# Moving the scaling of fifteen output columns from VectorE to GpSimd, with new splits of the last two row blocks

One core of one Trainium2 chip. The metric is the device time of one execution in microseconds (us); lower is better.

## The reference

```python
x: float32 [32, 512, 1024]; divisor = 1024.0
out = (np.sum(x, axis=-1) / divisor).astype(np.float32)      # [32, 512]
```

That is 16,384 sums of 1,024 floats. 67.11 MB are read and 0.07 MB written, so the kernel should cost what the input stream costs, plus a short tail behind the last bytes.

## The kernel before

Each of the 128 partitions holds 128 rows: 112 in the main part, then sixteen "last" ones. VectorE sums most rows with a reduce, ScalarE the others with an activation that accumulates. The loads get smaller towards the end: eight rows, four, two, then `row` (one row for each partition, shared between the two engines), then the last row in three pieces `pa`, `pb`, `pc`. All loads are on SyncE's queue. Cuts are marked `# ...`.

```python
    bulk = ctx.enter_context(tc.tile_pool(name="bulk", bufs=3))      # 14 rows each
    one = ctx.enter_context(tc.tile_pool(name="one", bufs=1))
    # ...
    res = one.tile([P, M], F32, name="res")          # M = 112 main rows
    fin = one.tile([P, L], F32, name="fin")          # L = 16 last rows
    q = one.tile([P, L], F32, name="q")
    r = one.tile([P, L], F32, name="r")
    nc.gpsimd.memset(r, 0.0)
    # ... main part; then loads and sums of 8, 4 and 2 rows into q (tiles t, t4, t2) ...
    c = 768
    row = one.tile([P, D], F32, name="row")
    load(row, x_last[:, j, :])
    act_sum(r[:, j : j + 1], row[:, c:], by=scale)                                   # ScalarE
    nc.vector.reduce_sum(out=q[:, j : j + 1], in_=row[:, :c], axis=AX)

    a, b = 448, 704
    pa = one.tile([P, a], F32, name="pa")
    pb = one.tile([P, b - a], F32, name="pb")
    pc = one.tile([P, D - b + 2], F32, name="pc")
    load(pa, x_last[:, L - 1, :a])
    load(pb, x_last[:, L - 1, a:b])
    load(pc[:, : D - b], x_last[:, L - 1, b:])
    # ... res scaled on GpSimd and stored ...
    act_sum(pc[:, D - b : D - b + 1], pa)                                            # ScalarE
    nc.vector.reduce_sum(out=pc[:, D - b + 1 :], in_=pb, axis=AX)
    nc.vector.scalar_tensor_tensor(
        out=fin[:, : L - 1], in0=q[:, : L - 1], scalar=scale, in1=r[:, : L - 1], op0=MULT, op1=ADD
    )
    scaled = one.tile([P, D - b + 2], F32, name="scaled")
    nc.vector.tensor_scalar(                                                         # "L198"
        out=scaled, in0=pc, scalar1=scale, scalar2=0.0, op0=MULT, op1=ADD, accum_out=fin[:, L - 1 :]
    )
    tc.keep_in_program_order(nc.sync.dma_start(out=o_last, in_=fin))
```

The sums of `pa` and `pb` are written behind the bytes of `pc`, so L198 scales and adds up everything of the last row. It therefore needs three things: pa's sum (ScalarE), pb's sum (VectorE) and pc's landing (DMA).

Two helpers run when the program is finished. `latest_wait_first` sorts the semaphore waits of an instruction; those that do not fit on it are asked for by an instruction ahead of it on the same sequencer. `close_while_storing` puts the checks of all other engines ahead of the last store.

```python
    def rank(i, w):
        own = {"DVE": "DVE_", "Activation": "Activation_", "SP": "DVE_", "Pool": "DVE_"}
        if w.ant_name.startswith("DMAHW") and i.engine != SP:
            return 0
        return 1 if w.ant_name.startswith(own.get(...)) else 2      # cut
```

## Time and profile before

| What | Before |
|---|---|
| median of 3 runs | 161.5 us (161.36 to 161.5) |
| span of the profiled run | 159.8 us |
| last landing of `row` | 156.16 us |
| last store issued | 158.31 us, 2.155 us after row's landing |

The span of the profiled execution, as the profile counts it, is 1.55 us shorter than its device time of 161.31 us. The time up to row's landing is the stream. The 2.155 us behind it are the tail, which is all that computation can still shorten. The page, the chain and the timeline of this kernel stand in the prediction below.

### The profile page before, as it was taken

What the parts mean: (1) busy time and instruction counts of PE and PEld (TensorE: products, weight loads), DVE (VectorE), ACT (ScalarE), POOL (GpSimd) and SP (SyncE); (2) the same over time, 40 slices, a digit from 0 to 9 for tenths busy, and PEclk for the clock granted to TensorE, in tenths of its full rate; (3) what the DMA queues carried; (4) which work ended last, traced back from release to release, by engine and by line L of the source; (5) the groups of instructions that cost most, each with busy time, mean ns of one, the idle gap of its engine ahead of it and who ended that gap; (6) DMA issues with size and microseconds to landing.
All of it is one profiled execution on the core that took longest, in us unless ns stands there. A gap on an engine that the chain in (4) does not pass through costs nothing.

```text
span 159.8 us, 139 instructions
## 1 busy us (share of the span) xinstructions
DVE 121.1 (76%) x17; ACT 19.6 (12%) x37; POOL 0.8 (0%) x6
## 2 busy tenths in 40 slices
DVE  0500059995999599978999599959995996494985
ACT  3000000000000000000000000000001900480973
POOL 0000000000000000000000000000000000001000
DMA  7999999978999999978999999978999999899993
GB/s 250 472 459 459 459 459 459 459 330 359 459 459 459 459 459 459 459 316 373 459 459 459 459 459 459 416 345 388 459 459 427 394 480 505 353 435 390 408 400 132
DMA packets 2592, 67.18 MB, mean 420 GB/s; under 512 B 544, under 2 KB 928, under 8 KB 1056
## 3 DMA queue, kind: packets, MB, share of 16 engines
q1 hardware_dynamic: 2592, 67.18, 98.0%
HBM read 67.11 MB, written 0.07 MB: 420 GB/s over the span
## 4 chain that ended last, share of the span: by engine, by line
DMA 76%; DVE 22%; SPq 1%; issue 0%; DVEq 0%
DMA t<-in_x_dram 56%; DMA row<-in_x_dram 21%; DVE res L153 20%; SPq L142 1%; DVE q L176 1%; DVE scaled L198 0%; DVE pc L193 0%; DVE fin L194 0%; DVEq L198 0%; DVEq L232 0%
## 5 line engine op out<-in xcount | busy, mean ns | idle before, releaser
L153 DVE TENSOR_REDUCE res<-t 128x14 f32<-128x14336 f32 (+3 forms) x9 | 111.2, 12360 | 34.3 <-DMA t<-in_x_dram 34.3
L147 ACT ACTIVATE junk<-t 128x1024 f32<-128x1024 f32 x16 | 16.2, 1013 | 135.9 <-DMA t<-in_x_dram 135.9
L153 DVE TENSOR_REDUCE q<-t 128x4 f32<-128x4096 f32 (+2 forms) x3 | 7.9, 2642 | 2.7 <-DMA t<-in_x_dram 2.5
L147 ACT ACTIVATION_READ_ACCUMULATOR junk<-t 128x1 f32 x16 | 3.0, 187 | 0.0
L147 ACT ACT_TABLE_LOAD x1 | 1.3, 1283 | 1.7 <-PEq L218 1.7
L189 POOL TENSOR_SCALAR res<-res 128x112 f32<-128x112 f32 x1 | 0.5, 494 | 143.8 <-DVE res L153 143.8
L176 DVE TENSOR_REDUCE q<-row 128x1 f32<-128x768 f32 x1 | 1.0, 953 | 0.0
L198 DVE TENSOR_SCALAR_CACHE_REDUCE scaled<-pc 128x322 f32<-128x322 f32 x1 | 0.5, 490 | 0.1
L147 ACT ACTIVATE junk<-pa 128x448 f32<-128x448 f32 x1 | 0.5, 548 | 0.0
L193 DVE TENSOR_REDUCE pc<-pb 128x1 f32<-128x256 f32 x1 | 0.4, 414 | 0.0
L147 ACT ACTIVATE junk<-row 128x256 f32<-128x256 f32 x1 | 0.4, 388 | 0.1
L194 DVE SCALAR_TENSOR_TENSOR fin<-q,r 128x15 f32<-128x15 f32 x1 | 0.2, 176 | 0.0
L147 ACT ACTIVATION_READ_ACCUMULATOR junk<-pa 128x1 f32 x1 | 0.2, 186 | 0.0
L147 ACT ACTIVATION_READ_ACCUMULATOR junk<-row 128x1 f32 x1 | 0.2, 185 | 0.0
L139 POOL MEMSET r<- 128x16 f32 x1 | 0.1, 112 | 1.3 <-POOLq L218 1.3
L218 POOL MEMSET const-bfloat16-1.0<- 128x1 bf16 x1 | 0.1, 103 | 0.0
L218 POOL MEMSET const-uint8-127<- 128x1 uint8 x1 | 0.1, 102 | 0.0
L218 POOL MEMSET const-float32-0.0<- 128x1 f32 x1 | 0.1, 99 | 0.2 <-issue 0.2
L218 POOL MEMSET const-float32-1.0<- 128x1 f32 x1 | 0.1, 99 | 0.0
L198 DVE DVE_READ_ACCUMULATOR scaled<-pc 128x1 f32 x1 | 0.1, 83 | 0.0
## 6 DMA issues: line engine op xcount, KB each, us to landing
t<-in_x_dram SPq DMA_DIRECT2D x7, 7168.0 KB, 35.7
t<-in_x_dram SPq DMA_DIRECT2D x1, 6144.0 KB, 33.3
t<-in_x_dram SPq DMA_DIRECT2D x1, 4096.0 KB, 26.1
t<-in_x_dram SPq DMA_DIRECT2D x2, 1024.0 KB, 18.6
t<-in_x_dram SPq DMA_DIRECT2D x1, 2048.0 KB, 30.5
row<-in_x_dram SPq DMA_DIRECT2D x1, 512.0 KB, 33.2
pa<-in_x_dram SPq DMA_DIRECT2D x1, 224.0 KB, 33.3
pc<-in_x_dram SPq DMA_DIRECT2D x1, 160.0 KB, 33.1
```

What stands on the lines that cost most here:

```text
L139: nc.gpsimd.memset(r, 0.0)
L142: tc.keep_in_program_order(nc.sync.dma_start(out=dst, in_=src))
L147: nc.scalar.activation(junk[:, :n], src, COPY, scale=by, accum_out=dst)
L153: nc.vector.reduce_sum(out=dst[:, :d], in_=t[:, :d, :], axis=AX)
L176: nc.vector.reduce_sum(out=q[:, j : j + 1], in_=row[:, :c], axis=AX)
L189: nc.gpsimd.tensor_scalar_mul(out=res, in0=res, scalar1=scale)
L193: nc.vector.reduce_sum(out=pc[:, D - b + 1 :], in_=pb, axis=AX)
L194: nc.vector.scalar_tensor_tensor(out=fin[:, : L - 1], in0=q[:, : L - 1], scalar=scale, in1=r[:, : L - 1], op0=MULT, op1=ADD)
L198: nc.vector.tensor_scalar(out=scaled, in0=pc, scalar1=scale, scalar2=0.0, op0=MULT, op1=ADD, accum_out=fin[:, L - 1 :])
L218: nc = _bacc.Bacc("TRN2", target_bir_lowering=False, num_devices=1)
```

## The change

Its intent: take the scaling of the fifteen columns out of VectorE's chain at the end, and re-split the last blocks so that VectorE gets less and ScalarE more. The memset of `r` is not needed any more, so `r` becomes one column.

```diff
-    r = one.tile([P, L], F32, name="r")
-    nc.gpsimd.memset(r, 0.0)
+    r = one.tile([P, 1], F32, name="r")
-    c = 768
+    c = 688
-    act_sum(r[:, j : j + 1], row[:, c:], by=scale)
+    act_sum(r, row[:, c:], by=scale)
-    a, b = 448, 704
+    a, b = 480, 672
-    nc.vector.scalar_tensor_tensor(
-        out=fin[:, : L - 1], in0=q[:, : L - 1], scalar=scale, in1=r[:, : L - 1], op0=MULT, op1=ADD
+    nc.gpsimd.tensor_scalar_mul(out=fin[:, :j], in0=q[:, :j], scalar1=scale)
+    nc.gpsimd.tensor_scalar(
+        out=fin[:, j : j + 1], in0=q[:, j : j + 1], scalar1=scale, scalar2=r, op0=MULT, op1=ADD
     )
```

## The prediction

> **What bounds the kernel now.** I read the page from the top, then the waits, then the end of the timeline and the landing records. The kernel sums 16,384 rows of 1,024 floats: 67.11 MB come in, 0.07 MB go out. The first thing to see is that the change cannot touch most of the span.
>
> ```profile
> span 159.8 us, 139 instructions
> DVE 121.1 (76%) x17; ACT 19.6 (12%) x37; POOL 0.8 (0%) x6
> q1 hardware_dynamic: 2592, 67.18, 98.0%
> HBM read 67.11 MB, written 0.07 MB: 420 GB/s over the span
> ```
>
> The DMA queue is busy for 98.0% of the span. VectorE (DVE) has 76%, ScalarE (ACT) 12%, GpSimd (POOL) under 1%. So the stream of input sets about 156 us, and what can be tuned is the tail behind the last loads. The chain that ended last, in order of time, shows how long that tail is (columns: start us, us, what):
>
> ```profile
> 122.91 33.25 DMA row<-in_x_dram
> 156.16 0.02 issue
> 156.18 0.96 DVE q L176
> 157.14 0.03 issue
> 157.17 0.18 DVE fin L194
> 157.34 0.34 DVE pc L193
> 157.68 0.04 DVEq L198
> 157.72 0.07 issue
> 157.79 0.49 DVE scaled L198
> 158.28 0.01 DVEq L232
> ```
>
> Here is the reader's main finding: from 156.18 to 158.28 VectorE runs without a real gap: the row ahead (L176), the scaling of fifteen columns (L194), the middle piece (L193), and the scaling with sum of the last piece (L198). Then SyncE issues the store at 158.31, which lands at 159.73; the span ends at 159.76. The landing records (the last of a load's sixteen increments) are: row 156.16, pa 156.70, pb 157.02, pc 157.50. So pb lay ready 0.24 us before VectorE began on it, and pc lay ready 0.29 us before L198 began. VectorE's own chain is late, not the data. ScalarE is not late either (timeline, ACT):
>
> ```profile
> 156.18 0.39 ACT L147 ACTIVATE junk<-row 128x256 f32<-128x256 f32 x1
> 156.50 0.18 ACT L147 ACTIVATION_READ_ACCUMULATOR junk<-row 128x1 f32 x1
> 156.72 0.55 ACT L147 ACTIVATE junk<-pa 128x448 f32<-128x448 f32 x1
> 157.20 0.19 ACT L147 ACTIVATION_READ_ACCUMULATOR junk<-pa 128x1 f32 x1
> ```
>
> Its last result is signalled at 157.40, also 0.39 us before L198. So the change has something to gain, but no more than the distance from 157.79 down to the next limit: pc at 157.50 plus the start of an instruction.
>
> **What the Trainium skill says.** (1) "VectorE: DVE Perf Modes", section "The perf-mode tier table": a reduce runs at one element a cycle. The trace agrees: 1,024 columns take 1,220 ns and 768 take 953 ns, a slope of 1.04 ns a column, with about 150 ns fixed. (2) "SBUF — State Buffer", section "Who interferes with whom": a VectorE instruction with two SBUF inputs contends with a GpSimd one that reads SBUF, while a reduce and the tensor_scalar form that writes out its accumulator do not. The tail of before has no GpSimd work, so no run yet shows it; but the 490 ns of L198 for 322 columns (322 x 1.04 = 335, plus 155) fits one element a cycle. The new GpSimd instructions should therefore delay nothing on VectorE, and the one two-input instruction there disappears. (3) "ScalarE: Activation LUTs", section "What ACT_TABLE_LOAD costs": an ACTIVATE with immediate scale and bias costs 186 ns + 0.833 ns a column. The trace has 388 ns for 256 and 548 ns for 448: exactly 0.833 ns a column, with 175 ns fixed; I use the trace. (4) "Perfetto Trace Analysis", section "GPSIMD Engine Instruction": a GpSimd instruction's reported span is unreliable. The trace cannot test that, so I leave its duration a wide margin below.
>
> **The change part by part.** I rebuild the tail from the landing of row at 156.16. The bytes ahead of it are the same, so I keep this time.
>
> Landings. pa grows by 32 columns (16 KB), pb shrinks by 64, pc grows by 32; the sum is the same. pb's 128 KB took 157.02 - 156.70 = 0.32 us, so 16 KB is 0.04 us. Hence pa lands at 156.74, pb at 156.98, and pc at 157.50 as before.
>
> VectorE. The row ahead has 688 columns instead of 768: 80 x 1.04 = 83 ns less, 870 instead of 953 ns, so it ends at 157.05. The scaling (L194) is gone: it held the chain for 0.18 us, and with it goes its 0.03 us start. In before, L193 could start 0.09 us before the end of the instruction ahead of it (157.26 against 157.34), as it had no wait on that one; now 157.05 - 0.09 = 156.96 comes before pb's landing, so pb's landing at 156.98 plus 0.02 for the start decides: 157.00. It reduces 192 columns: 414 - 64 x 1.04 = 347 ns, end 157.35, signalled 157.36.
>
> ScalarE. The row's part grows to 336 columns: 388 + 80 x 0.833 = 455 ns, and its accumulator is read by 156.76. pa landed at 156.74, so its ACTIVATE starts about 156.76, some 0.04 us later than before. It takes 548 + 32 x 0.833 = 575 ns, and by the spacing of before (start to signal 0.677 us, plus 0.027) the sum is signalled at about 157.465, 0.07 us later than before.
>
> The last instruction needs three things: pb's sum (157.36), pc's bytes (157.50) and pa's sum (157.465). In before it started 0.105 us after the signal of its last compute input (157.683 to 157.788). After: 157.465 + 0.105 = 157.57; for pc's landing 157.50 + 0.02 = 157.52. So L198 starts at 157.57, not 157.79: 0.22 us earlier. It handles 354 columns instead of 322: 32 x 1.04 = 33 ns more, 523 ns. It signals 0.54 us after its start, at 158.11, against 158.295. **Sum: 0.22 - 0.03 = 0.185 us gained**, and the fixed end (issue, store, closing) behind it is unchanged.
>
> The same by terms: removing L194 and the smaller row and pb would free about 0.32 us of VectorE time (157.465 against 157.79). ScalarE's larger shares take back 0.10 of it, as the pa sum becomes the last input, and the larger pc takes 0.03.
>
> GpSimd. The first new instruction (fourteen columns) needs nothing later than 156.15, the end of the reduce before the row. The second (one column, r as a per-partition scalar) needs the row's sum at 157.06. GpSimd started 0.08 us after such a signal in before (145.57 to 145.65), so at 157.14. The only size I have is this group:
>
> ```profile
> L189 POOL TENSOR_SCALAR res<-res 128x112 f32<-128x112 f32 x1 | 0.5, 494 | 143.8 <-DVE res L153 143.8
> ```
>
> As an upper estimate I take the full 494 ns for one column: done at about 157.65. The store needs it at 158.11, so 0.45 us of slack stay; even twice the estimate would cost only a few hundredths. The kernel's closing code makes SyncE check the other engines and the stored main result (landed 157.71) before the last store, which in before was passed at about 157.77. This is also under 158.11.
>
> At the other end the memset of r goes (112 ns at 1.7 us), beside a first load that lands at 4.8 us: worth nothing.
>
> **The rivals.** (A) GpSimd takes the place of L194 as the end of the chain. For: [...]a scalar read from memory, and a producer finishing at 157.06 only. Against: 0.45 us of slack and a 112-column instruction of the same kind at 494 ns. If the small one took 1.2 us, the store would leave at about 158.4 and the time would be 161.6, no gain. (B) The split was better before: ScalarE, which had 0.39 us to spare, becomes the limit. Partly this is already my reckoning. If pa's ACTIVATE also started 0.1 us later than I think, 0.08 us of gain are left: 161.4. (C) The transfer is the limit: pc lands at 157.50 in any case, so removing more VectorE work gives no more than about 0.27 us. If pc's landing slips by 0.1 us (other piece sizes; the tiles behind r also shift in memory as r shrinks from sixteen columns to one), the gain halves: 161.4. If ScalarE's sum comes sooner than reckoned, the limit is pc: 161.25. (D) GpSimd holds VectorE up through shared memory access: the second GpSimd instruction would lie over pb's reduce and the start of L198. The skill page speaks against it; if it delayed L198 until the end of the GpSimd instruction at 157.65, 0.1 us would remain: 161.4.
>
> **Range and chances.** Median before 161.5, minus 0.185: 161.3. All rivals lie between 161.25 and 161.6. The three runs of before lie 0.14 us apart, and the profiled run was at 161.31, so run-to-run noise is as large as the effect. I choose 161.0 to 161.6. A 2% change would be 3.2 us, more than the whole tail behind row's landing that computation fills (156.16 to 158.31 is 2.15 us); it would need the input stream itself to move, which nothing here does. So 0.98 for within 2% and 0.01 on each side.
>
> **What would show each step right or wrong.** In the profile after: the row's reduce near 870 ns and pb's near 347 ns; no VectorE scaling of fin; pb's reduce starting with its landing near 157.0; ACTIVATEs of about 455 and 575 ns; L198 of about 523 ns starting about 1.4 us after row's landing (before: 1.63); the store issued about 1.97 us after row's landing (before: 2.15); two small GpSimd instructions ending before L198 ends. It is wrong if the last store waits for GpSimd, if L198 begins later than 1.5 us after row's landing, or if row itself lands elsewhere than near 156.2, which would be a change of the stream that I see no cause for.

## The result, and the profile after

| | median | range | runs |
|---|---|---|---|
| before | 161.5 us | 161.36 to 161.53 | 4 |
| after | 161.57 us | 161.41 to 161.67 | 4 |

The ratio is 1.0005, with a 95% interval of 0.9988 to 1.0023. A ratio here is the mean time of one kernel's fast runs over that of the other's of the same rounds, so not quite the ratio of the medians. The time lies in the predicted range and in the "within 2%" class. The predicted gain of 0.185 us, though, is not there: 161.57 stands where 161.3 was expected. The question is where it went.

First the groups of the profile after (busy us, mean ns of one, then idle time before them and its releaser):

```profile
L188 POOL TENSOR_SCALAR res<-res 128x112 f32<-128x112 f32 x1 | 0.5, 496 | 145.4 <-DVE res L152 145.4
...
L175 DVE TENSOR_REDUCE q<-row 128x1 f32<-128x688 f32 x1 | 0.9, 870 | 0.1
L198 DVE TENSOR_SCALAR_CACHE_REDUCE scaled<-pc 128x354 f32<-128x354 f32 x1 | 0.5, 522 | 0.3 <-ACT junk L146 0.3
L146 ACT ACTIVATE junk<-pa 128x480 f32<-128x480 f32 x1 | 0.6, 574 | 0.1
L146 ACT ACTIVATE junk<-row 128x336 f32<-128x336 f32 x1 | 0.5, 455 | 0.2 <-DMA row<-in_x_dram 0.2
L192 DVE TENSOR_REDUCE pc<-pb 128x1 f32<-128x192 f32 x1 | 0.4, 354 | 0.1
L193 POOL TENSOR_SCALAR fin<-q 128x14 f32<-128x14 f32 x1 | 0.3, 262 | 10.2 <-DVE q L152 10.2
L194 POOL TENSOR_SCALAR fin<-q,r 128x1 f32<-128x1 f32 x1 | 0.3, 267 | 0.7 <-DVE q L175 0.7
```

Nearly every duration is as predicted: 870, 574 (575), 455, 522 (523) and 354 ns (347). The GpSimd instructions are cheaper than the allowance of 494 ns. What is new is in the line of L198: VectorE sat idle for 0.3 us before it, released by ScalarE. The chain that ended last says the same (start us, us, what):

```profile
123.56 33.65 DMA pa<-in_x_dram
157.21 0.02 issue
157.23 0.57 ACT junk L146
157.80 0.13 ACTq L232
157.93 0.03 issue
157.96 0.05 DVEq L198
158.01 0.08 issue
158.09 0.52 DVE scaled L198
158.61 0.01 DVEq L232
```

In before the chain ran from row's landing through four VectorE instructions. Now it comes from pa's landing through ScalarE. Between ScalarE's signal at 157.93 and L198 at 158.09 stand three pieces that add up to 0.16 us, more than the 0.11 us ahead of L198 in the chain of before. And one part of the page shows the stream (DMA issues: KB, us from issue to landing):

```profile
row<-in_x_dram SPq DMA_DIRECT2D x1, 512.0 KB, 33.4
pa<-in_x_dram SPq DMA_DIRECT2D x1, 240.0 KB, 33.6
```

Before it was 33.2 for row and 33.3 for pa. So both land 0.2 to 0.3 us later after their issue, though the bytes up to the end of row are the same. In the landing records row lands at 156.52, not 156.16, and the last store is issued at 158.64, 2.122 us after it. The tail is thus only 0.033 us shorter, and the stream ahead of it 0.365 us longer.

Half of these 0.365 us are in the first load, which the change does not touch: its last DMA engine was done at 4.98 us against 4.80. The first load's end varies from execution to execution (4.49 to 5.04 us in the fourteen profiles, 4.80 and 4.89 for the kernel of before; the two of the changed kernel are the latest, 4.98 and 5.04, and no run shows whether that is chance). The other half arises behind the eight-row load, where the tiles lie that stand behind `r` in memory.

In the trace's packet records (no view prints them) the same tiles look different. A load has one packet for each partition, eight on each DMA engine. In before, each of t4's 128 packets of 16 KB took 611 ns, with hardly an exception; in after they take 611 to 624 ns, on average 615.8. In the built programs t4 begins at byte 189,184 of a partition in before and at 189,152 in after: `r` shrank from 64 bytes to 4, which are padded to 32.

### The profile page after: what moved, and what is told of

Its sections match the earlier page's. It is cut to its first block, busy times and chain, and to the rows that moved or that the text cites. A ratio compares the mean times of both kernels' runs of the same rounds, so it can differ in the third digit from the quotient of the medians.

```text
span 160.1 us, 140 instructions
## 1 busy us (share of the span) xinstructions
DVE 120.9 (76%) x16; ACT 19.7 (12%) x37; POOL 1.2 (1%) x7
## 4 chain that ended last, share of the span: by engine, by line
DMA 77%; DVE 21%; SPq 1%; ACT 0%; issue 0%; ACTq 0%; DVEq 0%
DMA t<-in_x_dram 56%; DMA pa<-in_x_dram 21%; DVE res L152 20%; SPq L141 1%; ACT junk L146 0%; DVE scaled L198 0%; ACTq L232 0%; DVEq L198 0%; DVEq L232 0%
## 5 line engine op out<-in xcount | busy, mean ns | idle before, releaser
L175 DVE TENSOR_REDUCE q<-row 128x1 f32<-128x688 f32 x1 | 0.9, 870 | 0.1
L198 DVE TENSOR_SCALAR_CACHE_REDUCE scaled<-pc 128x354 f32<-128x354 f32 x1 | 0.5, 522 | 0.3 <-ACT junk L146 0.3
L146 ACT ACTIVATE junk<-pa 128x480 f32<-128x480 f32 x1 | 0.6, 574 | 0.1
L146 ACT ACTIVATE junk<-row 128x336 f32<-128x336 f32 x1 | 0.5, 455 | 0.2 <-DMA row<-in_x_dram 0.2
L194 POOL TENSOR_SCALAR fin<-q,r 128x1 f32<-128x1 f32 x1 | 0.3, 267 | 0.7 <-DVE q L175 0.7
L198 DVE DVE_READ_ACCUMULATOR scaled<-pc 128x1 f32 x1 | 0.1, 83 | 0.0
## 6 DMA issues: line engine op xcount, KB each, us to landing
t<-in_x_dram SPq DMA_DIRECT2D x1, 6144.0 KB, 33.3
pc<-in_x_dram SPq DMA_DIRECT2D x1, 176.0 KB, 33.3
```

The costliest lines, as they stand in the source:

```text
L146: nc.scalar.activation(junk[:, :n], src, COPY, scale=by, accum_out=dst)
L194: nc.gpsimd.tensor_scalar(out=fin[:, j : j + 1], in0=q[:, j : j + 1], scalar1=scale, scalar2=r, op0=MULT, op1=ADD)
L198: nc.vector.tensor_scalar(out=scaled, in0=pc, scalar1=scale, scalar2=0.0, op0=MULT, op1=ADD, accum_out=fin[:, L - 1 :])
```

## The experiments

**Theories.** M (place): the tiles behind `r` begin 32 bytes earlier, and each of their packets costs more; that eats the gain. S (spread): the sixteen DMA engines of an execution start unevenly, and that alone makes the difference. T (tail): the gain in the tail was never there, because GpSimd, ScalarE or the new split is late. Each run was timed in five rounds or more beside the kernel before, on the same chip. "Spacing" below is the mean landing of a load minus that of the load before it, divided by eight packets. "Tail" is the time from row's last landing to the issue of the last store. "Stretch" is the time from the median landing of the eight-row load (t8) to that of pc, and the first load's "spread" is the time between the first and the last of its sixteen landing signals. A packet of row is called long when it took over 180 ns.

### 1. before_again: the kernel of before, unchanged

> The unchanged kernel of before, for a second profile and for the noise of the comparison. All theories: ratio to before 1.000 with an interval of about 0.002 to either side. In the profile, theory M (place in memory) and theory S (the spread of the sixteen DMA engines, set in the first load of an execution) differ only if this execution begins with another spread than 0.354 us: M keeps the 4 KB packets of row at 159 ns and the stretch from the median landing of the eight-row load to that of pc at 9.91 us in any case; S lets both follow the spread (10.09 us at 0.53 us).

Measured: 161.34 us (before beside it 161.39), ratio 0.9998 (0.9986 to 1.0011). The first load's spread was 0.50 us this time, and still t4's packets took 611 ns each and the tail was 2.149 us. The stretch from t8 to pc was 9.80 us, shorter than the 9.91 of the first profile. There 16 of row's 128 packets had taken over 180 ns, here one. A wide spread alone does not bring the scatter: S is in trouble.

### 2. after_again: the changed kernel, unchanged

> The changed kernel once more. Theory M (tiles t4, t2, row, pa, pb, pc begin 32 bytes off a multiple of 64, as r shrank; each of their packets takes some ns longer): row's packets again scatter over 159 to 169 ns, mean 162, and the stretch from the eight-row load's median landing to pc's is again 10.09 us. Theory S (spread of the DMA engines in that execution): these follow the first load's spread and are back at 159 ns and 9.91 us if that is near 0.35 us. Time: 161.5, ratio 1.000.

Measured: 161.68 us (161.55 to 161.79) against 161.39, ratio 1.0020 (1.0007 to 1.0032): slightly slower, clear of the noise. t4's packets again took 612 to 624 ns and the stretch was 10.09 us. The tail was 2.112 us. My number for the time (161.5) was too low; the profile came out as M says.

### 3. after_aligned: the changed kernel with `r` wide again

```diff
-    r = one.tile([P, 1], F32, name="r")
+    r = one.tile([P, L], F32, name="r")[:, :1]
```

> The changed kernel with r again sixteen columns wide in memory (one used), so all tiles behind it begin where they did before; nothing else differs. Theory M: row's packets 159 ns without scatter, stretch 9.91 us, the last store issued about 1.97 us after row's landing, time 161.3, ratio to before 0.9988. Theory S: no difference from the changed kernel beyond what the first load's spread makes; ratio 1.000. A third theory (the tail's gain never was there: the GpSimd or ScalarE result is late by itself) has the last store still 2.1 us after row's landing although packets are at 159 ns.

Measured: 161.34 us, ratio 0.9997 (0.9984 to 1.0011). t4's packets are back at 611 ns, so the place made the scatter; and as this execution's first load had a spread of 0.60 us, the widest but one of all fourteen, S falls as the cause of the scatter. (For the stretch it is not excluded; see what stays open.) The profiled execution was unlucky: 37 of row's packets took 186 to 424 ns, the stretch was 10.09 us for this reason and this execution took 161.75; the other four took 161.22 to 161.46. The tail was 2.064 us. That is better than 2.155 but not the 1.97 of the prediction. So the third theory holds a part: some of the tail's gain was never there. (`pa` is 128 bytes longer than in before, so pb and pc begin 128 bytes later than there, here and in split_only; t4, t2, row and pa are where they were.)

### 4. before_shifted: the kernel of before with its tiles moved by 32 bytes

```diff
-    r = one.tile([P, L], F32, name="r")
+    r = one.tile([P, L + 8], F32, name="r")
```

> The kernel of before with r eight columns wider than needed, so t4, t2, row, pa, pb and pc begin 32 bytes off a multiple of 64; nothing else differs. Theory M: row's packets scatter, mean about 162 ns, stretch 10.09 us, time 161.5 + 0.18 = 161.7, ratio 1.001. Theory S: as before, 161.5, with 159 ns and 9.91 us unless the first load's spread is large.

Measured: 161.53 us, ratio 1.0011 (0.9999 to 1.0024), t4's packets 615.0 ns on average, stretch 10.09 us, tail unchanged at 2.148 us. The computation is that of before and only the place differs, and the packets and the stretch are as in after. The time alone does not prove it: its interval reaches 1.

### 5. split_only: the new splits, the scaling still on VectorE

```diff
-    c = 768
+    c = 688
-    a, b = 448, 704
+    a, b = 480, 672
```

> The kernel of before with the new splits alone (row 688 to 336; last row 480, 192, 352); the fifteen columns stay on VectorE, tiles begin on multiples of 64 bytes. Worked out from the profiles: the scaling on VectorE follows the row's reduce, pb's reduce starts 1.01 us after row's landing, its sum is there at 1.37, ScalarE's at about 1.37, L198 at 1.48 us, the last store 2.04 us after row's landing (before 2.15). Time about 0.1 us under before, ratio 0.9993, inside the noise. Rival (the split costs nothing by itself, GpSimd does): 2.0 us or less.

Measured: 161.25 us against 161.33, ratio 0.9996 (0.9983 to 1.0008), tail 2.091 us. The split by itself takes 0.06 us off the tail, less than the 0.11 expected, because pa landed 0.666 us after row, ScalarE's sum came last at 1.393 (1.37 expected), and L198 began 0.141 us after that instead of the 0.11 I had used (see experiment 11).

### 6. gp_only_aligned: the scaling on GpSimd, the old splits, no tile moved

```diff
 # against after_aligned
-    c = 688
+    c = 768
-    a, b = 480, 672
+    a, b = 448, 704
```

> GpSimd does the fifteen columns, but the splits are those of before (768 to 256; 448, 256, 320) and r stays sixteen columns wide, so no tile moves. If the larger ScalarE share of the new split is what eats the gain: pb's sum is there 1.30 us after row's landing, ScalarE's at 1.24 as before, L198 starts at 1.41, the last store is issued at 1.94 us after row's landing, 0.13 us sooner than in after_aligned (2.06), ratio about 0.9987. If GpSimd itself is late or holds VectorE up: 2.06 or more.

Measured: 161.09 us (161.04 to 161.28) against 161.33, ratio 0.9986 (0.9973 to 0.9998), tail 1.955 us (1.94 expected). This is the gain that the prediction looked for, and without the new split. Its chain (start us, us, what) is VectorE's again, with the piece "DVE fin" gone:

```profile
156.15 0.95 DVE q L175
157.10 0.34 DVE pc L192
157.44 0.04 DVEq L198
157.48 0.08 issue
157.56 0.49 DVE scaled L198
158.04 0.01 DVEq L232
```

GpSimd was at work on its one column while VectorE reduced pb; the reduce took 416 ns against 411 and 414 in the two profiles of before. So GpSimd's one column costs pb's reduce a few ns at most.

### 7. tuned: GpSimd, no tile moved, splits for three inputs at once

```diff
 # against after_aligned
-    c = 688
+    c = 736
-    a, b = 480, 672
+    a, b = 448, 688
```

> GpSimd does the fifteen columns, r wide (no tile moves), row 736 to 288, last row 448, 240, 336, so that the three inputs of L198 come together: pa's sum 1.24, pb's sum 1.27, pc's landing 1.34 us after row's landing. L198 then starts at 1.38 and the store is issued at 1.92 us after row's landing (before 2.15). Time 0.2 us under before, ratio 0.9986, the best of all. If the splits do not matter: same as gp_only_aligned or after_aligned within 0.03 us in the profile.

Measured: 161.11 us, ratio 0.9986 (0.9974 to 0.9999), tail 1.953 us. The three inputs come within 0.05 us of each other (1.267, 1.299, 1.313 us after row), yet nothing is won over the old splits: what L198 gains in its start, it loses with sixteen more columns.

### 8. before_all_shifted: every tile moved by 32 bytes

```diff
+    pad = ctx.enter_context(tc.tile_pool(name="pad", bufs=1))
+    gap = pad.tile([P, 8], F32, name="gap")
+    nc.gpsimd.memset(gap, 0.0)
     bulk = ctx.enter_context(tc.tile_pool(name="bulk", bufs=3))
```

> The kernel of before with a 32-byte tile allocated ahead of all others, so every load's tile begins 32 bytes off a multiple of 64. Theory M, if the cost is a few ns for each packet whatever its size (4.4 ns at 16 KB): 81 packets more of the large loads on each DMA engine, +0.36 us, besides the 0.3 us of before_shifted: 162.0, ratio 1.004. If it grows with the bytes (0.7% at 16 KB): +1.0 us and more, 162.6, ratio 1.007. Theory S (no effect of the place): 161.4, ratio 1.000.

Measured: 161.50 us against 161.33, ratio 1.0008 (0.9994 to 1.0022). That is no more than before_shifted, and again the interval reaches 1. I had expected the large loads to suffer too, by 0.36 us at least; they did not. Their spacing was 1,816.6 ns for 48 KB packets here and 1,816.8 in before. My form of M, "a few ns for each packet that is off 64 bytes", was wrong for the large tiles.

### 9. before_shifted64: the tiles behind `r` moved by 64 bytes

```diff
-    r = one.tile([P, L], F32, name="r")
+    r = one.tile([P, L + 16], F32, name="r")
```

> The kernel of before with r sixteen columns wider, so t4 and the tiles behind it move by 64 bytes: still multiples of 64, no longer of 128 or 256. If a multiple of 64 is enough: packets 611.3 (16 KB), 74 (pa) and 55 ns (pc) without scatter, stretch 9.80 us, ratio 1.000. If it takes 128 or 256: as before_shifted, 615 ns, 55 to 68 ns, stretch 10.09 us, ratio 1.001.

Measured: 161.38 us against 161.2, ratio 1.0007 (0.9993 to 1.0021). The outcome is mixed, and it tells most. t4's packets are back at 611 ns (median), as with a multiple of 64. But t4's spacing is 612.8 ns, as in the shifted kernels. (The time and the stretch of the profile, 10.38 us, also hold 40 long packets of row, so I read only t4's and t2's spacing.)

| Kernel | t4 begins at, modulo 256 | t4 packet, mean ns | t4 spacing, ns | t2 spacing, ns |
|---|---|---|---|---|
| before_again | 0 | 611.3 | 604.0 | 303.7 |
| gp_only_aligned | 0 | 611.3 | 604.0 | 304.6 |
| after_aligned | 0 | 611.7 | 604.1 | 305.6 |
| before_shifted | 32 | 615.0 | 612.3 | 312.6 |
| before_all_shifted | 32 | 614.7 | 612.4 | 312.0 |
| before_shifted64 | 64 | 612.1 | 612.8 | 310.7 |
| after_again | 224 | 615.8 | 612.9 | 312.1 |

So 32 and 224 make the packets' own times scatter, but each of the three places tried that is not a multiple of 256 costs 8 to 9 ns for each 16 KB packet in what counts, the spacing. Over all profiles, t4's spacing is 603.8 to 606.8 ns in the nine with t4 at a multiple of 256 and 612.3 to 613.1 in the five others, whatever the first load's spread. For t2 (8 KB) the distance is less clear: 303.3 to 309.5 against 310.7 to 312.6. In the three moved kernels of before, pa and pb show it too, with 5 to 8 ns over before and before_again, but pc hardly (53.5 to 54.1 ns against 51.4 and 53.7).

This would also explain experiment 8. The large tiles begin at 16,512 in every other kernel, which is 128 modulo 256: they are off already, so a move by 32 bytes need not make it worse. Two estimates speak for that. The first is from the traces alone: in before, packets of 56, 48 and 32 KB came every 2,117.6, 1,816.8 and 1,214.1 ns. These lie on a line with 9.4 ns at no bytes, and at 16 KB this line is at 611.8 ns, near t4's spacing when it is moved and 8 ns above the 604.0 at a multiple of 256. The second is from the Trainium skill, "DMA: Bandwidth & Descriptors", section "Where 436 GB/s comes from", which has a ceiling of 435.2 GB/s for sixteen ports, so 27.2 GB/s for each. (The section adds that the HBM side, about 358 GB/s, limits loads from HBM; here the 56 KB packets came at 433 GB/s in all, so the measurement speaks for the higher ceiling.) By that, 16 KB take 602.4 ns, and t4's spacing at a multiple of 256 is 1.6 ns above; 48 KB take 1,807.1 ns, and the large tiles' spacing in before is 9.7 ns above. By both estimates the two groups of tiles differ by about 8 ns within one kernel. No run put the large tiles at a multiple of 256, so this is argued and not shown.

### 10. after_aligned_2: after_aligned once more

> after_aligned once more, since its profiled execution was the slowest of its five by 0.3 us and 37 of row's packets took 186 to 424 ns. Where the places of the tiles alone are the extra cost: packets 611.3, 159, 79, 36 and 60 ns, stretch from the eight-row load's median landing to pc's 9.80 us, the last store 2.06 us after row's landing (its heavier ScalarE share costs 0.11 us against gp_only_aligned), time 0.09 us under before, ratio 0.9994. If the tail's gain is not there at all: ratio 1.000 and 2.15 us.

Measured: 161.08 us against 161.2, ratio 0.9990 (0.9978 to 1.0003), tail 2.027 us. t4's packets 611 ns; the stretch was 9.92 us with 13 long packets of row. The four kernels of this kind (3, 10, 11, 12) have ratios of 0.9997, 0.9990, 0.9995 and 0.9995, all under 1 and each within its own noise; the tail's 0.09 to 0.14 us would be 0.9991 to 0.9994.

### 11. after_order: two waits of L198 in the other order

```diff
 # against after_aligned
-        own = {"DVE": "DVE_", "Activation": "Activation_", "SP": "DVE_", "Pool": "DVE_"}
+        own = {"DVE": "Activation_", "Activation": "Activation_", "SP": "DVE_", "Pool": "DVE_"}
```

> after_aligned with the order of two waits ahead of L198 swapped: VectorE's own sum (pb) is asked for first, ScalarE's (pa), which comes last here, second. L198 began 0.153 us after pa's signal in all profiles where pa's sum is last and was asked for first, 0.105 us after pb's where that is last and asked for second. If the order is the cause, 0.105 here, and the last store 2.01 us after row's landing, 0.05 us sooner than after_aligned; time too little to tell. If it comes from something else in a late ScalarE sum: again 0.15 us.

Measured: ratio 0.9995 (0.9982 to 1.0009), tail 2.008 us. The timelines of after_aligned_2 and of this kernel (start us, us, engine, line, operation), first after_aligned_2:

```profile
157.02 0.19 ACT L146 ACTIVATION_READ_ACCUMULATOR junk<-pa 128x1 f32 x1
157.37 0.52 DVE L198 TENSOR_SCALAR_CACHE_REDUCE scaled<-pc 128x354 f32<-128x354 f32 x1 [0.20 <-DMA pc<-in_x_dram]
```

and after_order:

```profile
157.50 0.19 ACT L146 ACTIVATION_READ_ACCUMULATOR junk<-pa 128x1 f32 x1
157.80 0.52 DVE L198 TENSOR_SCALAR_CACHE_REDUCE scaled<-pc 128x354 f32<-128x354 f32 x1 [0.19 <-DMA pc<-in_x_dram]
```

From the start of the accumulator's reading to L198 it is 0.35 us there and 0.30 us here. By the semaphore records L198 started 0.147 us after pa's signal there, and 0.141 to 0.154 in all six profiles in which pa's sum is the later of the two and asked for first (split_only's 0.141 is one of them, so the 0.153 "in all profiles" of the expectation was misread); here it was 0.111 us. The record of VectorE's sequencer shows the step: with pa asked for first, its waiting instruction begins 0.027 us after pa's signal and takes 0.050 us more; with pa asked for last, it is over 0.035 us after the signal. In both cases L198 begins 0.06 to 0.08 us after that. So the order makes the difference, in the one profile that has it: the wait that ends last should be asked for last. (Both lines name pc's landing as the releaser of L198. But L198 starts 0.122 and 0.098 us after that landing, while row's reduce, which waits for a landing alone, starts 0.02 us after it. Where several inputs come within 0.03 us of each other, the view's choice means little.)

### 12. gp_twice_aligned: one more GpSimd instruction ahead of the last

```diff
 # against after_aligned
+    extra = one.tile([P, 1], F32, name="extra")
+    nc.gpsimd.tensor_scalar(out=extra, in0=q[:, j : j + 1], scalar1=scale, scalar2=r, op0=MULT, op1=ADD)
     nc.gpsimd.tensor_scalar(
         out=fin[:, j : j + 1], in0=q[:, j : j + 1], scalar1=scale, scalar2=r, op0=MULT, op1=ADD
```

> after_aligned with one more GpSimd instruction of the same kind (0.27 us, result unused) ahead of the last one. If GpSimd has the slack that the prediction gave it: nothing changes, last store 2.06 us after row's landing, ratio 0.9994. If GpSimd's result is what the last store waits for, or it holds VectorE up: 0.1 to 0.3 us later.

Measured: ratio 0.9995 (0.9983 to 1.0007), tail 2.039 us, between the two of after_aligned. From its timeline:

```profile
157.27 0.26 POOL L195 TENSOR_SCALAR extra<-q,r 128x1 f32<-128x1 f32 x1 [0.82 <-DVE q L175]
157.41 0.19 ACT L146 ACTIVATION_READ_ACCUMULATOR junk<-pa 128x1 f32 x1
157.51 0.27 POOL L196 TENSOR_SCALAR fin<-q,r 128x1 f32<-128x1 f32 x1
...
158.31 0.34 SPq L203 DMA_DIRECT2D out_dram<-fin  x1
```

GpSimd ends at 157.77, half a microsecond before the store, even with the work doubled. The two starts are 0.24 us apart, so here the reported 0.26 us is right to within 0.02 us.

## Why the prediction was right, and where it was wrong

The range and the class were right, and so was the reason for the class: the tail is too short for 2%. That the median lies in the range is in part luck: 161.57 is 0.03 us from its end, and after_again's median, 161.68, is outside. The direction was wrong. Two of the prediction's own signs of being wrong came true: L198 began 1.564 us after row's landing (1.5 was the limit), and row landed at 156.52 and not near 156.2. Step by step:

1. **"the scaling (L194) is gone", worth about 0.2 us: right**, shown alone by gp_only_aligned (tail 1.955 against 2.149 and 2.155 us, ratio 0.9986).
2. **GpSimd has slack: right.** In after it ended 1.26 us after row's landing (1.49 allowed for), 0.86 us before the store. Rivals A and D fell, by experiments 12 and 6.
3. **Durations of VectorE and ScalarE: right**, all within 7 ns (pb's reduce took 354 ns in after, and the predicted 347 in split_only, where no GpSimd instruction runs beside it).
4. **"The bytes ahead of it are the same, so I keep this time": this step failed.** The same bytes went to tiles that no longer began at multiples of 256 bytes. From the spacings of t4, t2 and row in the profiles of after and before_again: 8 x (613.1 - 604.0) + 8 x (312.6 - 303.7) + 8 x (161.8 - 154.4) = 0.20 us. That alone cancels the predicted 0.185. (These are two profiles; t2's and row's share varies between profiles, t4's hardly.) Rival C named the shift as a possibility and sized it at 0.1 us, on pc's landing only; it acts on the loads from the four-row one to pb, and pc's own spacing hardly changes.
5. **"Hence pa lands at 156.74", 0.58 us after row: too early.** It was 0.684 in after and 0.674 in after_again. Part of the error is again the place: with the old pa, moving the tiles took this landing from 0.54 to between 0.58 and 0.62 us. The rest is that a larger pa costs more than the 0.04 us I took for its 16 KB: with pa in place it is 0.596 to 0.625 in four profiles. Split_only, also in place, has 0.666, so how the error divides is not shown. Rival B was right in kind: ScalarE became the last input.
6. **"it started 0.105 us after the signal of its last compute input": mis-sized here.** It was 0.153 us in after by the semaphore records, as ScalarE's wait is asked for first. Experiment 11 shows the order to be the cause.

Steps 5 and 6 add up: L198 was expected 1.41 us after row's landing and came at 1.564; 0.10 us are pa's landing, 0.05 the waits. So the tail gained 0.03 to 0.04 us in place of 0.185, and the stream lost about 0.2. The split, put in to help, gives back 0.07 to 0.11 us of GpSimd's gain even with t4, t2, row and pa in place (2.027 to 2.064 against 1.955).

What stays open: why a place off 256 costs a nearly fixed 8 ns; whether the large tiles, at 128 past a multiple of 256, pay it too; whether the scatter in packet times costs anything by itself; and what lengthens row's packets in some executions. In those with 37 and 40 long packets row came (by mean landings) 0.2 to 0.4 us later behind the two-row load than in those with none to five, which is as much as any effect or more, and one reason to read tails and spacings and not times alone. A wide spread of the first load may have a part in it: of the kernels with t4 in place, the two with the widest (0.60 and 0.61 us, after_aligned and gp_twice_aligned) have the most long packets (37 and 21) and a stretch of 10.09 and 10.11 us, as long as in after. But before_shifted64 has 40 at 0.42 us, and no run changes the spread alone. Also, after_again took 0.15 us more than before_shifted (161.68 against 161.53), though its tail is 0.04 us shorter; in the two profiles the first load ended 0.08 us later and row landed 0.10 us later, and no run tells whether the change has a part in that.

The best version that was run is gp_only_aligned, 0.14% under before; tuned is its equal. An estimate from the spacings, not run: the ten loads into the large tiles have 80 packets on each engine, so moving those tiles by 128 bytes might be worth up to 80 x 8 ns = 0.6 us. That run would also test whether the large tiles pay at all.

## What to carry to other kernels

When a change shrinks or adds a small tile, look at where the tiles behind it begin: here a 16 KB packet cost 8 to 9 ns more at each of three places (32, 64 and 224 bytes past a multiple of 256) than at a multiple of 256. When work moves from one engine to another at a join, recompute which input is last, and ask for that one last. Test the parts of a bundled change one by one; here the best part was hidden by the other two.

## What the Trainium skill lacked or had wrong

- "DMA: Bandwidth & Descriptors", section "How a descriptor splits into AXI transactions": a start off a 256-byte boundary costs the beats from the boundary to the start. It agrees that 256 is the boundary, but by its count an offset of 32, 64 or 224 bytes would waste 1, 2 or 7 beats (an estimate: 1.2 to 8.2 ns at the page's 32 bytes and 850 MHz); the runs show 8.3, 8.8 and 8.9 ns more for each 16 KB packet over 604.0, hardly dependent on the offset. By its rule for the first transaction, though, a 16 KB packet takes 65 transactions instead of 64 at any of these offsets, which would fit a cost that hardly depends on the offset; no run tests that. The page speaks of fetching; what moved here is the written side, in SBUF, on which no page that I read gives a time.
- No page that I read gives the cost of the order of two waits on a sequencer: 0.141 to 0.154 us from the last engine's signal to the start when it is asked for first (six profiles), 0.111 us when it is asked for last (one profile).
- No page that I read gives GpSimd's time for a tiny tensor_scalar: 262 ns for 14 columns, 267 ns for one with a per-partition scalar, 496 ns for 112.
